# Moving three two-by-two up pairs one block earlier and giving their taps and gate product later

## The chip, the cores and the metric

The kernel runs on one core of one Trainium2 chip. The metric is the device time of one execution in microseconds; several executions are timed and their median is compared. One further execution is recorded by the hardware profiler, and all rows below come from that one.

## The reference, cut to what matters

The program is one block of a gated hybrid encoder on 512 positions of width 1024, all in float32. The change lies in the channel mixer at its end:

```python
h = rms_norm(x, norm_ffn_g[l])
up = causal_dwconv(h @ w_up[l], conv_ffn_w[l])      # w_up: 1024 x 5632, three taps per channel
a, b = jnp.split(up, 2, axis=-1)                    # two halves of 2816
x = x + (jax.nn.silu(a) * b) @ w_down[l]            # w_down: 2816 x 1024
...
return rms_norm(x, norm_f_g)
```

## The kernel before, in words

Everything is held transposed: 128 channels on the partitions, 512 positions along the row. Float32 products are made from three matmuls in a rounded format. Each weight chunk `raw` is read by DMA, ScalarE writes its rounded high part `wh` (L279), VectorE writes the rest `wl = raw - wh` (L283), and TensorE computes `wh*xh`, `wh*xl` and `wl*xh`. `split()` issues this for one chunk. There are two buffers for `wh` and two for `wl`, so the split of a chunk can start when TensorE has left the chunk two places before it. Five buffers hold `raw`.

The chunks are used in one fixed order, the list `stream`. `chunk.n` counts those that TensorE has been given, `len(parts)` those that have been split. The names in the list are `up<m>` (one plain up block of 128 columns, 48 matmuls), and `P<n>` and `F<n>` (the first and second part of one step of a two by two scheme with seven products, 18 and 24 matmuls).

The 5632 up columns are taken in pairs `j` = 0 to 21: block `2j` is a piece of `a`, block `2j+1` the piece of `b` that it is multiplied with. Most pairs are two plain up blocks (`block`, 96 matmuls). The pairs named in `UPS` go by the two by two scheme instead (`up_pair`): four chunks P, F, P, F with 84 matmuls, whose products land in four PSUM banks `us`, and five VectorE sums (L1099 to L1104) that put the two blocks together. The scheme needs weights that are sums of blocks; these are made in DRAM by a chain of six DMAs a group (copy, add, copy, add, copy, add: L140 on SyncE's queue, L143 on GpSimd's queue). The DMAs of all groups stand in the list `todo`, and `tick()` issues the next one; `ticks(name)` says how many go with the split of each chunk. The F chunks are then loaded from these sums. Pairs 0 to 11 are the first half, pairs 12 to 21 the second; after each half `down` multiplies what has been made with `w_down`.

After each block or pair, `up` scales the result by the norm (`z`, L1122 and L1120) and applies the three taps: a ScalarE copy (L615) and two VectorE additions (L616, L619) into a tile `fu`, of which there are three buffers. `glu` then applies SiLU to `a` (L1132) and multiplies by `b` on GpSimd: into `ge` for an even `j` (L1135) and into `go` for an odd `j` (L1142). After an odd `j`, the sums and splits of the result that `down` needs (L1152 to L1157, L1161, L1162) are put in the list `later` with a chunk at which they are due. `run_later` takes from that list at each split as much as a budget allows: 1.7 us at an up chunk, and 0.45 us at a P or F chunk of an up pair, which none of these entries fits. `flush()` issues what is left, and `glu` calls it for every odd `j`.

An instruction is put into its engine's queue by a planner, which takes among those ready by its own reckoning the one that stands first in the program. `keep` holds the order of matmuls and DMAs as written; `after_split()` puts what is issued under it behind the newest split on ScalarE and on VectorE. Each engine works its queue off strictly in order.

The last pair of `UPS` has a further duty: behind it the space of the x sums is free, the running result `x1` is read back into it (`xg`, L1109), and later pairs put `z` there (`fz`) and not in PSUM. A copy of a piece of `x1` (L1343) is queued on ScalarE behind that read.

Of the kernel before, what the change touches and what calls it, by code (L numbers as in the profile page):

```python
# [8 lines left out]
F32 = mybir.dt.float32  # L9
# [4 lines left out]
P = 128  # L14
D = 1024
S = 512
# [18 lines left out]
G1, G2, GF, BG, CM, CF, BF = 0, 8, 16, 24, 40, 52, 184  # L35
# [17 lines left out]
)  # L53
GS = 2
NFF = len(STEPS[0]) + len(STEPS[1])
UPS = (3, 7, 13, 16, 19)
NUP = NFF + 2 * (8 - GS)
MIXED = (4, 2, 4, 4, 2, 4, 2)

# [5 lines left out]
def block_kernel(ctx, tc, xT, vecs, wv, win, wmix, wo, wup, wst, wdp, outT):  # L65
# [56 lines left out]
    for (j0, j1), n0, n1 in zip(PHASES, (0, len(STEPS[0])), (len(STEPS[0]), NFF - 1)):  # L122
        groups += [[NUP + 2 * i, NUP + 2 * i + 1] for i, j in enumerate(UPS) if j0 <= j < j1]
        groups += [list(range(n, min(n + 2, n1))) for n in range(n0, n1, 2)]
    groups.append([NFF - 1])
    nstep = [len(d) for d in STEPS[0] + STEPS[1]] + [2] * (2 * (KB - GS) + 2 * len(UPS))
    todo = []
# [40 lines left out]
    def up_n(j):  # L168
        return [NUP + 2 * UPS.index(j) + d for d in range(2)]

# [14 lines left out]
    for ph, (j0, j1) in enumerate(PHASES):  # L185
        for j in range(j0, j1):
            if j in UPS:
                for m in up_n(j):
# [9 lines left out]
    raws, parts, order = [], [], {}  # L198
# [3 lines left out]
    def after_split():  # L202

        st = ExitStack()
        for ins in order.values():
            st.enter_context(tc.issue_after(ins))
        return st

    def load(upto):
        for k in range(len(raws), min(upto, len(stream) - 1) + 1):  # L210
            nm, src, ncol = stream[k]
            if held[0] == NRAW:
                return
            held[0] += 1
            raw = wp.tile([P, D], F32, tag="raw", name=f"raw_{nm}", bufs=NRAW)
            if k == 0:

                keep(nc.scalar.dma_start(raw[:, :VW], src[:, :VW]))
                keep(nc.sync.dma_start(raw[:, VW:ncol], src[:, VW:]))
            else:  # L220
                keep(nc.sync.dma_start(raw[:, :ncol], src))
            raws.append(raw[:, :ncol])
# [31 lines left out]
    def split(hl=None):  # L254

        k = len(parts)
        if k == len(stream):
            return
        nm, _, ncol = stream[k]
        load(k + (LOOK if k >= gs0 else AHEAD))  # L260
        if k >= gs0:
            for _ in range(ticks(nm)):
                tick()
        if hl is None:
            hl = []
            for x in "hl":
                if k == 0:
                    wp.tile([P, PADW[x]], F32, tag=f"pad{x}", name=f"pad_{x}")
                hl.append(wp.tile([P, D], F32R, tag=f"w{x}", name=f"w{x}_{nm}", bufs=2)[:, :ncol])
        hi, lo = hl  # L270
        raw = raws[k]
        if k < 2:
            if k:
                keep(nc.scalar.activation(hi[:, :VW], raw[:, :VW], AF.Copy))
            else:
                keep(nc.vector.tensor_copy(hi[:, :VW], raw[:, :VW]))
            keep(nc.vector.tensor_copy(hi[:, VW:], raw[:, VW:]))
        else:
            ins = nc.scalar.activation(hi, raw, AF.Copy)  # L279
            order["hi"] = ins.ins  # L280
            if k < KB:
                keep(ins)
        ins = nc.vector.tensor_sub(lo, raw, hi.bitcast(F32))  # L283
        order["lo"] = ins.ins
        if k < KB:
            keep(ins)
        held[0] -= 1
        parts.append((hi, lo))
        run_later(k, 0.45 if nm[0] in "PF" and int(nm[1:]) >= NUP else {"u": 1.7, "P": 1.6, "F": 0.75, "d": 0}.get(nm[0], 3.5))
# [323 lines left out]
    def taps(u, z, w):  # L613

        nc.scalar.activation(u, z, AF.Copy, scale=col(w + 2))  # L615
        nc.vector.scalar_tensor_tensor(  # L616
            u[:, 1:], z[:, : S - 1], col(w + 1), u[:, 1:], op0=ALU.mult, op1=ALU.add
        )
        nc.vector.scalar_tensor_tensor(  # L619
            u[:, 2:], z[:, : S - 2], col(w), u[:, 2:], op0=ALU.mult, op1=ALU.add  # L620
        )
# [116 lines left out]
    z, e, o = (ap.tile([n, S], F32, tag="pp", name=nm, bufs=NPP) for nm in ("fz", "fe", "fo"))  # L738
# [156 lines left out]
    for j in range(KB):  # L895
# [28 lines left out]
        a, b = gs  # L924
# [44 lines left out]
    def block(name, xh, xl, lead=False):  # L969
        wh, wl = chunk(name)  # L970
        q = acc(f"p_{name}")
        for kb in range(KB):
            ks = slice(kb * P, (kb + 1) * P)
            if lead and kb < 2:
                if kb:
                    passes([
                        (q[:, cs], 0, wh[:, b], wl[:, b], xh[:, a, cs], xl[:, a, cs], True, False)
                        for a, b in enumerate((slice(0, P), ks)) for cs in halves
                    ], 4)
                continue  # L980
            mm3(q, wh[:, ks], wl[:, ks], xh[:, kb, :], xl[:, kb, :], kb == 0, kb == KB - 1)
        return q
# [54 lines left out]
    nrm = {}  # L1037
# [13 lines left out]
    pu = lead(["up0", "up1"], x1h, x1l, mid)  # L1051
# [7 lines left out]
    fp = ctx.enter_context(tc.tile_pool(name="fp", bufs=1))  # L1059
# [13 lines left out]
    def fz(name):  # L1073
        fz.n += 2
        a = 2 * KB + fz.n % (2 * KB)
        return xg[:, a : a + 2].rearrange("p h c -> p (h c)")
# [11 lines left out]
    def up_pair(j):  # L1088
# [8 lines left out]
        with after_split():  # L1097
# [6 lines left out]
            nc.vector.tensor_add(p45h, p45h, u.unsqueeze(1).to_broadcast([P, 2, S // 2]))  # L1104
        if j == UPS[-1]:
            xg = xfp.tile([P, 4 * KB, 2 * P], F32, tag="xf", name="xg")
# [2 lines left out]
                nc.gpsimd.dma_start(x1[:, a : a + 4, :], x1d[:, a : a + 4, :])  # L1109
        return p23, p45  # L1110

    def up(j, rb2, pu=None):
        uu = []
        if j in UPS:
            pu = up_pair(j)
        for s_ in range(2):
            p = pu[s_] if pu else block(f"up{2 * j + s_}", x1h, x1l, True)
            z = p if j <= UPS[-1] else fz(f"fz{j}{s_}")
            if s_ and j in UPS:
                nc.vector.scalar_tensor_tensor(z, p, -1.0, rb2, op0=ALU.mult, op1=ALU.mult)  # L1120
            else:
                nc.vector.tensor_mul(z, p, rb2)  # L1122
            u = fp.tile([P, S], F32, tag="fu", name=f"fu{j}{s_}", bufs=3)
            taps(u, z, CF + 3 * (2 * j + s_))
            uu.append(u)
        return uu

    def glu(ph, j, uu):
        a, b = uu
        q, k = j // 2, len(parts) - 1  # L1130
        g0 = place(ph, q)
        nc.scalar.activation(a, a, AF.Silu)  # L1132
        if j % 2 == 0:
            ge = glu.even = fp.tile([P, 2, 2 * P], F32, tag="ge", name=f"ge{q}", bufs=2)
            keep(nc.gpsimd.tensor_mul(ge, a.rearrange(halves_of, h=2), b.rearrange(halves_of, h=2)))  # L1135
            return
        flush()
        ge = glu.even
        go = fp.tile([P, 6, 2 * P], F32, tag="gr", name=f"go{q}")

        def mul(eng):
            return eng.tensor_mul(go[:, 0:2, :], a.rearrange(halves_of, h=2), b.rearrange(halves_of, h=2))  # L1142

        if j + 1 < PHASES[ph][1]:
            keep(mul(nc.gpsimd))
        else:
            later.append((k + 3, 0.7, (("q", q),), lambda: mul(nc.vector)))
        b11, b12 = ge[:, 0, :], ge[:, 1, :]
        b21, b22, t1, t2, t3, t4 = (go[:, i, :] for i in range(6))

        def t13():
            nc.vector.tensor_sub(t1, b11, b12)  # L1152
            nc.vector.tensor_sub(t3, b22, b12)

        def t24():
            nc.vector.scalar_tensor_tensor(t2, t1, -1.0, b22, op0=ALU.mult, op1=ALU.subtract)
            nc.vector.scalar_tensor_tensor(t4, t2, -1.0, b21, op0=ALU.mult, op1=ALU.subtract)  # L1157

        def hl(src, gs):
            def f():  # L1160
                nc.scalar.activation(gh[:, gs, :], src, AF.Copy)  # L1161
                nc.vector.tensor_sub(gl[:, gs, :], src, gh.bitcast(F32)[:, gs, :])  # L1162

            return f


        d = (2, 3, 4) if j + 1 < PHASES[ph][1] else (4, 5, 6)
        w = [(d[0], 0.85, t13), (d[0], 0.85, t24), (d[1], 0.7, hl(ge[:, : 1 + ph, :], slice(g0, g0 + 1 + NF * ph, NF)))]
        w += [(d[x > 0 and 2 or 1], 0.7, hl(go[:, x : x + 2, :], slice(g0 + 1 + x, g0 + 3 + x))) for x in (0, 4, 2)]
        for n, us, f in w:  # L1170
            later.append((k + n, us, (("q", q),), f))
# [126 lines left out]
    for ph, (j0, j1) in enumerate(PHASES):  # L1298
        if ph:
            flush()  # L1300
            acc = ring(*X, *Y)
        for j in range(j0, j1):
            glu(ph, j, up(j, nrm["b"], None if j else pu))
        down(ph, ph * len(STEPS[0]))


# [210 lines left out]
```

## Time and profile before

| | |
|---|---|
| median of 3 runs | 694.88 us (693.62 to 694.9) |
| profiled execution | 693.69 us, of which the span from the first to the last instruction is 691.9 us |
| mean granted TensorE clock | 0.997 |
| busy: PE, DVE, ACT, POOL | 681.3, 548.3, 364.5, 184.6 us (98%, 79%, 53%, 27%) |
| PE waits recorded from the second half's first up block to the start of its `down` | 2.7, 0.4 and 0.2 us |

PE is TensorE, PEld its weight load, DVE VectorE, ACT ScalarE, POOL GpSimd, SP SyncE; a q behind the name means the engine's queue of DMAs and semaphores. Times in rows are us from the start of the span. A row of the timeline has the start, the length, the engine, the line, the operation, what it writes and reads, the tile sizes and how many instructions were merged; in brackets the idle time before it and what ended that. Instructions are pipelined, so the time that one of a row of equals really takes is the distance from its start to the next start, which is a little less than its length.

### The profile page before, as it was taken

To read this page: it belongs to the slowest core of one execution; us is meant where nothing else is said; L and a number is where in the kernel's file an instruction comes from. 1 tells how busy PE (TensorE), PEld (TensorE's weight loads), DVE (VectorE), ACT (ScalarE), POOL (GpSimd) and SP (SyncE) were. 2 spreads that over 40 slices of the span, in tenths; PEclk is the share of its full clock that TensorE was granted. 3 is DMA by queue.
4 is the path that set the end of the run, shared out by engine and by line. 5 is a ranking of instruction groups with operands and counts; after the bars stand their busy time and mean duration, and the time that the engine had idled before them with its cause. 6 is when DMAs were issued, how large, how long until landed. Compare 5 with 4: busy or idle time off the path is not lost.

```text
span 691.9 us, 14692 instructions
## 1 busy us (share of the span) xinstructions
PE 681.3 (98%) x5916; PEld 678.7 (98%) x5916; DVE 548.3 (79%) x864; ACT 364.5 (53%) x581; POOL 184.6 (27%) x209
## 2 busy tenths in 40 slices
PE   9999999999999999999999999999999999899996
PEld 9999999999999999999999999999999999899996
DVE  6678777886687777768887989978755899799886
ACT  6575556564564544446654535445443455355663
POOL 5123745444021010233403132330221323123000
PEclk9999999999999999999999999999999999999998
DMA  8626957478489796888975869679899968594623
GB/s 302 201 86 218 207 144 184 100 179 169 126 222 286 212 262 206 236 263 275 215 208 140 219 129 303 169 198 266 208 300 300 231 162 204 119 312 111 198 82 122
DMA packets 66117, 139.64 MB, mean 202 GB/s; under 512 B 5856, under 2 KB 30432, under 8 KB 65792
## 3 DMA queue, kind: packets, MB, share of 16 engines
q1 hardware_dynamic: 44592, 105.72, 46.8%
q0 software_dynamic: 20736, 32.28, 26.5%
q8 instruction: 46, 0.75, 0.4%
q10 hardware_dynamic: 720, 0.69, 0.3%
q14 instruction: 23, 0.19, 0.1%
HBM read 132.32 MB, written 49.81 MB: 263 GB/s over the span
## 4 chain that ended last, share of the span: by engine, by line
PE 86%; DVE 8%; ACT 3%; issue 2%; DMA 1%; ACTq 0%; SPq 0%; DVEq 0%
PE p_up L312 17%; PE p_in L312 14%; PE dn L330 13%; PE gs L330 8%; PE p_wo L312 6%; PE us L330 6%; PE p_up L330 5%; PE yc L330 3%; PE ya L312 3%; PE o L705 2%; PE pa L524 2%; PE pb L526 1%; PE tp L690 1%; PE pdB L312 1%; PE pdA L312 1%
## 5 line engine op out<-in xcount | busy, mean ns | idle before, releaser
L143 POOL DMA_DIRECT2D sum<-in_wst_dram x66 | 70.9, 1227 | 96.1 <-DMA sum<-sum 67.6
L312 PE MATMUL p_in<-xf,wh_in 128*128 128x256 f32 x576 | 95.7, 278 | 0.0
L312 PE MATMUL p_up<-x1h,wh_up 128*128 128x256 f32 x416 | 81.1, 276 | 0.0
L312 PEld LDWEIGHTS p_in<-xf,wh_in 128*128 128x128 f32 x576 | 80.4, 188 | 0.7
L312 PE MATMUL p_up<-x1h,wl_up 128*128 128x256 f32 x416 | 81.0, 276 | 0.0
L312 PE MATMUL p_up<-x1l,wh_up 128*128 128x256 f32 x416 | 81.0, 276 | 0.0
L279 ACT ACTIVATE wh_F<-raw_F 128x1024 fp32r<-128x1024 f32 (+1 forms) x42 | 44.2, 1052 | 65.0 <-PE ya L312 25.8
L283 DVE TENSOR_TENSOR wl_F<-raw_F,wh_F 128x1024 fp32r<-128x1024 f32 (+1 forms) x42 | 53.5, 1275 | 28.6 <-ACT wh_F L279 28.3
L312 PEld LDWEIGHTS p_up<-x1h,wh_up 128*128 128x128 f32 x416 | 62.7, 188 | 0.0
L312 PEld LDWEIGHTS p_up<-x1h,wl_up 128*128 128x128 f32 x416 | 62.6, 188 | 0.0
L312 PEld LDWEIGHTS p_up<-x1l,wh_up 128*128 128x128 f32 x416 | 62.6, 188 | 0.0
L312 PE MATMUL p_in<-xf,wl_in 128*128 128x256 f32 x288 | 56.6, 278 | 0.1
L279 ACT ACTIVATE wh_P<-raw_P 128x768 fp32r<-128x768 f32 (+1 forms) x42 | 35.1, 836 | 39.6 <-PE p_up L312 17.9
L279 ACT ACTIVATE wh_up<-raw_up 128x1024 fp32r<-128x1024 f32 x34 | 35.9, 1057 | 28.6 <-PE p_up L312 14.1
L283 DVE TENSOR_TENSOR wl_up<-raw_up,wh_up 128x1024 fp32r<-128x1024 f32 x34 | 42.3, 1244 | 9.5 <-ACT wh_up L279 9.4
L283 DVE TENSOR_TENSOR wl_P<-raw_P,wh_P 128x768 fp32r<-128x768 f32 (+1 forms) x42 | 40.1, 956 | 11.5 <-ACT wh_P L279 6.0
L312 PEld LDWEIGHTS p_in<-xf,wl_in 128*128 128x128 f32 x288 | 43.6, 188 | 0.3 <-DVE wl_in L283 0.3
L1135 POOL TENSOR_TENSOR ge<-fu,fu 128x512 f32<-128x512 f32 x11 | 20.1, 1825 | 82.3 <-DVE fu L619 44.7
L330 PE MATMUL dn<-gh,wh_F 128*128 128x256 f32 x156 | 36.5, 277 | 0.4 <-ACT wh_F L279 0.4
L330 PE MATMUL dn<-gl,wh_F 128*128 128x256 f32 x156 | 36.4, 276 | 0.0
L283 DVE TENSOR_TENSOR wl_in<-raw_in,wh_in 128x1024 fp32r<-128x1024 f32 x24 | 30.2, 1257 | 6.1 <-ACT wh_in L279 3.4
L1142 POOL TENSOR_TENSOR go<-fu,fu 128x512 f32<-128x512 f32 x9 | 12.6, 1396 | 72.9 <-DVE fu L619 54.5
(361 smaller groups left out, 2122.1 us busy)
## 6 DMA issues: line engine op xcount, KB each, us to landing
raw_F<-sum SPq DMA_DIRECT2D x41, 512.0 KB, 5.4
raw_up<-in_wup_dram SPq DMA_DIRECT2D x34, 512.0 KB, 5.4
raw_P<-in_wst_dram SPq DMA_DIRECT2D x41, 384.0 KB, 5.1
raw_in<-in_win_dram SPq DMA_DIRECT2D x24, 512.0 KB, 3.6
sum<-in_wst_dram POOLq DMA_DIRECT2D x41, 256.0 KB, 6.9
sum<-in_wst_dram SPq DMA_DIRECT2D x20, 512.0 KB, 8.6
sum<-in_wst_dram POOLq DMA_DIRECT2D x20, 512.0 KB, 9.1
sum<-sum SPq DMA_DIRECT2D x40, 256.0 KB, 6.2
```

The lines of the kernel that those rows point to most:

```text
L143: return lambda: keep(nc.gpsimd.dma_start(dst, src, accum_op=ALU.add))
L279: ins = nc.scalar.activation(hi, raw, AF.Copy)
L283: ins = nc.vector.tensor_sub(lo, raw, hi.bitcast(F32))
L312: keep(nc.tensor.matmul(out[:, cs], w, x[:, cs], start=start and i == 0 and c == 0, stop=stop and i == 2 and c == len(cut) - 1,))
L330: keep(nc.tensor.matmul(out, wl if x == 1 else wh, xl if x == 2 else xh, start=opens and bk not in seen, stop=closes and bk not in left,))
L524: keep(nc.tensor.matmul(pa[t][:, :VW], xt, w[:, :VW], start=start, stop=stop))
L526: keep(nc.tensor.matmul(pb[t], xt, w[:, VW:], start=start and t % 2 == 0, stop=stop and t % 2 == 1))
L690: keep(nc.tensor.transpose(tp[:, ks], pt[:, ks], ident))
L705: keep(nc.tensor.matmul(o[:, os_], vv[:, kb, pr, e, :], x[:, kb, cs], start=e == 0 and kb == 0 and i == 0, stop=e == 1 and kb == nk - 1 an ...
L1135: keep(nc.gpsimd.tensor_mul(ge, a.rearrange(halves_of, h=2), b.rearrange(halves_of, h=2)))
L1142: return eng.tensor_mul(go[:, 0:2, :], a.rearrange(halves_of, h=2), b.rearrange(halves_of, h=2))
```

## The change

Three things are changed. In the second half the pairs that go by the two by two scheme are 12, 15 and 18 and no longer 13, 16 and 19; so four plain blocks stand between two of them as before, none stands ahead of the first, and six stand behind the last. For these three pairs, `up` makes `z` (in PSUM, in place) and stops; taps, SiLU and the gate product are put in `held_up`. They are issued in the next pair's `up`, behind its first block's matmuls, after splits have been issued up to the third chunk behind the up pair, and behind that split on ScalarE and VectorE. And `glu` is called from inside `up`.

```diff
-UPS = (3, 7, 13, 16, 19)
+UPS = (3, 7, 12, 15, 18)
...
-    def up(j, rb2, pu=None):
+    def up(ph, j, rb2, pu=None):
         uu = []
         if j in UPS:
             pu = up_pair(j)
         for s_ in range(2):
             p = pu[s_] if pu else block(f"up{2 * j + s_}", x1h, x1l, True)
+            if s_ == 0 and held_up:
+                while len(parts) < chunk.n + 2:
+                    split()
+                with after_split():
+                    held_up.pop()()
             z = p if j <= UPS[-1] else fz(f"fz{j}{s_}")
             if s_ and j in UPS:
                 nc.vector.scalar_tensor_tensor(z, p, -1.0, rb2, op0=ALU.mult, op1=ALU.mult)
             else:
                 nc.vector.tensor_mul(z, p, rb2)
-            u = fp.tile([P, S], F32, tag="fu", name=f"fu{j}{s_}", bufs=3)
-            taps(u, z, CF + 3 * (2 * j + s_))
-            uu.append(u)
-        return uu
+            if j not in UPS or not ph:
+                z = tapped(j, s_, z)
+            uu.append(z)
+        if j in UPS and ph:
+            held_up.append(lambda: glu(ph, j, [tapped(j, s_, z) for s_, z in enumerate(uu)]))
+        else:
+            glu(ph, j, uu)
+
+    held_up = []
+
+    def tapped(j, s_, z):
+        u = fp.tile([P, S], F32, tag="fu", name=f"fu{j}{s_}", bufs=3)
+        taps(u, z, CF + 3 * (2 * j + s_))
+        return u
...
         for j in range(j0, j1):
-            glu(ph, j, up(j, nrm["b"], None if j else pu))
+            up(ph, j, nrm["b"], None if j else pu)
```

## The prediction

> **What bounds the kernel now.** I read the page's busy shares first, then the chain of work that ended last over the second half's up blocks, then TensorE's (PE's) waits there.
>
> ```profile
> PE 681.3 (98%) x5916; PEld 678.7 (98%) x5916; DVE 548.3 (79%) x864; ACT 364.5 (53%) x581; POOL 184.6 (27%) x209
> ```
> ```profile
> 523.84 1.36 PE p_up L330 x12
> ...
> 600.70 9.52 PE us L330 x84
> ...
> 632.31 1.37 PE dn L330 x12
> ```
> ```profile
> PE p_up L330 <- DVE wl_up L283: 2.7, 1, 2.7
> ```
> PE is the bound: an undisturbed up pair takes 9.52 us for 84 matmuls, 0.1133 us each. The stage from 523.84 to 632.31 has 14 plain blocks of 48 and three pairs of 84, 924 matmuls, so 104.7 us of work; it lasts 108.5. About 3.75 us are lost in it. PE's timeline shows where:
>
> ```profile
> 567.77 0.28 PE L330 MATMUL us<-xf,wl_P 128*128 128x256 f32 x1
> 568.22 0.39 PE L330 MATMUL us<-x1h,wh_F 128*128 128x256 f32 x1 [0.17 <-ACT wh_F L279]
> 587.50 0.28 PE L330 MATMUL p_up<-x1l,wh_up 128*128 128x256 f32 x1
> 590.43 0.75 PE L330 MATMUL p_up<-x1h,wl_up 128*128 128x256 f32 x4 [2.65 <-DVE wl_up L283]
> 591.02 0.28 PE L312 MATMUL p_up<-x1h,wh_up 128*128 128x256 f32 x1
> 627.17 0.28 PE L330 MATMUL p_up<-x1l,wh_up 128*128 128x256 f32 x1
> 627.41 0.73 PE L330 MATMUL p_up<-x1h,wl_up 128*128 128x256 f32 x4
> 633.51 0.84 PE L330 MATMUL dn<-gh,wl_P 128*128 128x256 f32 x6
> 634.79 0.39 PE L330 MATMUL dn<-gh,wh_F 128*128 128x256 f32 x1 [0.44 <-ACT wh_F L279]
> ```
> Starts stand 2.93 us apart at 587.50 where 0.11 would do; with the slower restart (0.59 us for four) this stop costs 2.96. The others cost 0.45 (568.22), 0.25 (627.41, with its restart) and 0.7 (634.79, just behind the stage). Together 4.4 us: all that can be won here. The large one is at up36, the third block behind pair 16. VectorE's (DVE's) queue, and the split's ScalarE (ACT) half, say why:
>
> ```profile
> 577.50 0.42 DVE L1099 TENSOR_TENSOR uz<-us,uz 128x256 f32<-128x256 f32 x1
> 577.83 0.68 DVE L1162 TENSOR_TENSOR gl<-ge,gh 128x512 fp32r<-128x512 f32 x1
> 578.43 0.42 DVE L1100 TENSOR_TENSOR uu<-us,uz 128x256 f32<-128x256 f32 x1
> ...
> 582.69 0.69 DVE L1122 TENSOR_TENSOR p_up<-p_up,rb_n 128x512 f32<-128x512 f32 x1
> 583.28 1.40 DVE L616 SCALAR_TENSOR_TENSOR fu<-us,vec,fu 128x511 f32<-128x511 f32 x2
> 584.60 1.40 DVE L619 SCALAR_TENSOR_TENSOR fu<-us,vec,fu 128x510 f32<-128x510 f32 x2
> 585.91 0.74 DVE L616 SCALAR_TENSOR_TENSOR fu<-p_up,vec,fu 128x511 f32<-128x511 f32 x1
> ...
> 589.16 1.21 DVE L283 TENSOR_TENSOR wl_up<-raw_up,wh_up 128x1024 fp32r<-128x1024 f32 x1
> 590.30 0.74 DVE L616 SCALAR_TENSOR_TENSOR fu<-p_up,vec,fu 128x511 f32<-128x511 f32 x1
> ```
> ```profile
> 581.51 1.06 ACT L279 ACTIVATE wh_up<-raw_up 128x1024 fp32r<-128x1024 f32 x1 [2.98 <-issue]
> ```
> The high part was there at 582.57, yet DVE first did 582.69 to 589.16: the pair's four taps (583.28 to 585.91, 2.63 us), other taps and gate work. DVE is full for long:
>
> ```profile
> 544.10:566.10 22.00, 22.00 (x197) 22.00 (x196) 21.24 (x32) 10.15 (x16) 5.41 (x4) 1.00 0.82 204
> 576.00:600.60 24.60, 21.95 (x193) 21.75 (x193) 21.31 (x33) 10.49 (x17) 5.27 (x5) 1.00 0.59 127
> ```
> (The columns are stretch, length, and busy PE, PEld, DVE, ACT, POOL; then clock and DMA.) In the four blocks behind a pair, 21.8 us of PE work, DVE has 21.2 and 21.3 us of its own. So order within DVE's queue decides.
>
> **The change, part by part.** No matmul is added or removed; the granted clock is 1.00 in these rows. Undisturbed, pair 12 would run 523.84 to 533.36, four blocks to 555.12, pair 15 to 564.64, four blocks to 586.40, pair 18 to 595.92 and six blocks to 628.56.
>
> *The held taps.* The third block's split now stands ahead of the pair's taps and of all that follows them. At up36 that alone puts `wl` at some 582.7 and ready by 583.9, when it is first used about 587.8. I take the 2.96 us as gone (bounds: all of it, or all but 0.3, since the pair's own 2.63 are surely out of the way). This adds a wait: DVE can't touch the taps until the third block's high part is made. That part ends 5.44 + 1.06 = 6.5 us behind the pair. Pair 16, which ended at 576.0, had its sums begun 1.5 behind that (577.50); sums and products took 5.2 to 582.69 with three `gl` of 0.60 among them (577.83 to 578.43), 3.4 without. So behind pair 12 DVE stands idle about 1.6 us; behind 15 and 18 gate sums fill that. It costs nothing, since no gate sums are due in the four blocks behind pair 12; without that cover the first split of pair 15 would be up to 1.6 late. Queued behind are only taps, whose results nothing on PE needs before `down`; the banks they leave late (two of eight) are taken again a pair later.
>
> *The fourth block.* Its split comes behind the held taps and one block's `z` and taps: with 0.60 and 0.66 each (starts 582.69, 583.28, 584.60) that is some 4.5 us behind the third split, so ready about 1.6 us ahead of use. Nothing lost; two late microseconds would cost 0.4.
>
> *Six plain blocks at the end.* DVE gets 32.6 us behind pair 18 where it had 21.8 behind pair 19, with the same work. The stops at 627.41 and 634.79 (0.95 us) should go. The cover is slack in DVE; without it both stay.
>
> *Pair 12 first.* Its loads move ahead by two chunks; its sums' last DMA is still issued some 24 chunks earlier. Four split pieces and `combine`'s last five small sums fall into 9.5 us of an otherwise empty DVE: nothing.
>
> *Where it hurts: pair 18.* The gate sums of pairs 12/13 come due at chunks of pair 15, where the budget of 0.45 us takes none, so they wait for up32 and up33. Those of 14/15 come due at pair 18's chunks and are flushed by `glu(17)`, ahead of pair 18's first split P40. So two gate loads fall between pairs 15 and 18; between pairs 13 and 16 there was one.
>
> ```profile
> 539.71 2.17 DVE L283 TENSOR_TENSOR wl_F<-raw_F,wh_F 128x1024 fp32r<-128x1024 f32 x1 [0.44 <-ACT wh_F L279]
> ...
> 564.88 0.94 DVE L283 TENSOR_TENSOR wl_P<-raw_P,wh_P 128x768 fp32r<-128x768 f32 x1
> 565.75 0.74 DVE L619 SCALAR_TENSOR_TENSOR fu<-p_up,vec,fu 128x510 f32<-128x510 f32 x1
> ...
> 574.90 0.41 DVE L1152 TENSOR_TENSOR go<-ge 128x256 f32<-128x256 f32 x1
> 575.24 0.41 DVE L1153 TENSOR_TENSOR go<-go,ge 128x256 f32<-128x256 f32 x1
> ```
> ```profile
> 539.51 1.29 POOL L1135 TENSOR_TENSOR ge<-fu,fu 128x512 f32<-128x512 f32 x1 [10.40 <-DVE fu L619]
> ```
> Work between up32's split (high part ready at 561.92 + 1.06, about 563.0) and the end of P40's: four splits of 1.14 (589.16 to 590.30) and one of 0.87 (564.88 to 565.75), 5.4; two gate loads of four sums at 0.34 and four `gl` at 0.60, 7.5; pair sums and two products 3.4 (577.50 to 582.69 less three `gl`); pair taps 2.6; three `z` at 0.60 and six taps at 0.66, 5.8. Sum 24.7, so 587.7. P40's rest is wanted after 12 of its matmuls, 586.40 + 1.36 = 587.76. No slack; on top come up35's `z` (0.6, its bank is full by then) and collisions with GpSimd: a split of usually 1.23 us took 2.17 while a gate product ran, 0.94 more, and two products (`go` 15, `ge` 16) fall into this stretch. I take one collision: a new stop of 1.5 us; bounds 0 (no collision, no `z`) and 3.4 (both, so 2.4, and 1.0 where F40's high part has to queue behind a late SiLU, as the one at 568.22 may have).
>
> The Trainium skill ("SBUF — State Buffer", section "SBUF: two separate sides") says that VectorE with two SBUF inputs and GpSimd lock the port pair they share, and that the loser blocks for the whole instruction. The 2.17 us split agrees: it came 0.2 us behind the product and lasted until 1.1 us behind its end. By that rule both products would cost their full 1.29 here; the new stop would be 3.1 us and the time 693.6.
>
> *x1's read.* It moves from the end of pair 19, 610.2, to that of pair 18, 595.9.
> ```profile
> 621.23 0.42 ACT L1343 ACTIVATE gh<-xg 128x256 fp32r<-128x256 f32 x1 [2.53 <-DMA xg<-x1d]
> ```
> ACT stood 2.53 us in front of that copy. The wait will come again, some 14 us sooner; taps are behind it, and six blocks cover them: 0, or 0.9 if it delays up41's split past its slack of 1.6.
>
> *Sum.* 4.4 won, 1.5 lost: 2.9 us. The profiled execution was 693.69 us, 1.8 over its span; it would be 690.8. The median, 694.88, lies 1.2 above it; less 2.9 that is **692.0 us**.
>
> **Rivals.** *The stop only moves.* All of the upper bound at pair 18, plus the late read: 4.4 - 3.4 - 0.9, so 694.8. For it: DVE has as much work as before, and two gate loads meet. Against: one gate load ahead of pair 16 cost 0.45 at 568.22, and the second one has 9.5 us of pair 15 in which DVE can catch up on all else.
>
> *The full lock.* Both products, 2 x 1.29 (539.51), block DVE for their whole length in the stretch that has no slack: 587.7 + 0.6 + 2.6 is 3.1 late, 4.4 - 3.1 won, 693.6. The rule of the Trainium skill's page above is this case. Against: the one row that shows it has 0.94 and not 1.29.
>
> *It doesn't do what it says:* the planner queues other work ahead of the third split. No change, 694.9. Against: the split now stands first in the program, and ACT's half was on time at 582.57.
>
> *Slower.* GpSimd (POOL) works its queue in order. The last sum DMAs of the groups behind pair 18's move up to three chunks later, and the held `go` 15 product is now behind them. Each such add waits for a copy to land.
> ```profile
> POOL sum L143 <- DMA sum<-sum: 67.6, 6, 22.1
> ```
> The last of them waits for a copy that SyncE issues behind the load of P40, when F39's split has freed a buffer, near 562. `fu` has three buffers, so up33's taps wait for `go` 15, and ACT and DVE queue P40's split behind those taps. From about 578 on each late microsecond costs one; 16 us are there, but 22.1 has been waited. At 22 the stop grows by 6: 698. Pair 18's own sums, whose last add comes near 560, are wanted only at 586.
>
> **How the numbers follow.** Chances: forecast 0.65, stop moves 0.13, lock 0.09, nothing done 0.05, slower 0.08. A measurement of this kernel tells 0.2% (1.4 us) from no change: 693.5 divides faster from same. The forecast's cases are nearly all faster, the three after it mostly same. The forecast's own bounds: 4.4 won without a new stop, 690.5, and 694.88 - 1.0 = 693.9. One run in three stood 1.3 below the median, so I reach to 689.8 below and, towards the stop that moves, to 694.6 above.
>
> **What the profile would show.** Right: PE's wait for `wl_up` at the third block gone behind all three pairs, the pair's L616 and L619 behind a `wl_up`, stage end near 630 and no wait at `down`'s first F; a stop of one to two microseconds at P40. Wrong: a stop at P40 or F40 above 3 us, POOL waiting in L143 ahead of `go`, or a DVE idle behind each pair for the held split.

## The result, and the profile after

The changed kernel takes 690.71 us (median; 690.7 to 691.35) against 694.9 us for the kernel before beside it (693.62 to 695.24). The ratio is 0.9944, 95% interval 0.993 to 0.9959. The profiled execution took 690.7 us with a span of 688.9, against 693.69 and 691.9. So the profiles differ by 3.0 us and the medians by 4.2: two amounts, with two causes.

The busy shares, the chain that ended last over the second half's `up` and its `down`, and PE's waits there, all of the kernel after:

```profile
PE 680.0 (99%) x5916; PEld 677.8 (98%) x5916; DVE 547.3 (79%) x864; ACT 364.6 (53%) x581; POOL 184.2 (27%) x209
```
```profile
523.78 9.52 PE us L330 x84
...
555.07 6.13 PE us L330 x54
561.22 1.07 ACT wh_up L279
...
577.22 1.31 POOL go L1157
...
587.72 0.88 DVE wl_P L283
588.65 8.45 PE us L330 x72
...
629.74 15.30 PE dn L330 x135
```
```profile
PE us L330 <- DVE wl_P L283: 0.9, 1, 0.9
```
The stage now lasts from 523.78 to 629.74, 105.96 us; before it lasted 108.47. The single recorded wait for `wl_up` at the third block behind a pair is gone. In its place stands one shorter wait at P40, pair 18's first chunk. From 629.74 `down` runs 135 matmuls without a break, so the stop at its first F is gone as well. The chain tells where the new wait comes from: between 561.22 and 588.65 it leaves PE and runs through DVE for the most part, with pieces on ACT and one product on POOL. In that stretch DVE's queue sets the end, and elsewhere in the stage PE does.

PE at the new stop and where the fourth block behind pair 18 first uses its low part, and DVE's queue at three places (behind pair 12, ahead of P40, behind pair 18):

```profile
587.32 0.39 PE L330 MATMUL us<-xf,wh_P 128*128 128x256 f32 x2
588.65 0.50 PE L330 MATMUL us<-x1h,wl_P 128*128 128x256 f32 x2 [0.94 <-DVE wl_P L283]
...
614.16 0.62 PE L330 MATMUL p_up<-x1h,wl_up 128*128 128x256 f32 x4
```
```profile
538.78 0.70 DVE L1127 TENSOR_TENSOR p_up<-p_up,rb_n 128x512 f32<-128x512 f32 x1 [0.25 <-PE p_up L312]
539.87 1.23 DVE L283 TENSOR_TENSOR wl_up<-raw_up,wh_up 128x1024 fp32r<-128x1024 f32 x1 [0.39 <-ACT wh_up L279]
...
577.60 0.75 DVE L619 SCALAR_TENSOR_TENSOR fu<-p_up,vec,fu 128x510 f32<-128x510 f32 x1
578.25 1.35 DVE L283 TENSOR_TENSOR wl_up<-raw_up,wh_up 128x1024 fp32r<-128x1024 f32 x1
...
582.11 1.22 DVE L1168 TENSOR_TENSOR go<-go,ge 128x256 f32<-128x256 f32 x1
...
587.64 0.95 DVE L283 TENSOR_TENSOR wl_P<-raw_P,wh_P 128x768 fp32r<-128x768 f32 x1
588.51 0.69 DVE L1127 TENSOR_TENSOR p_up<-p_up,rb_n 128x512 f32<-128x512 f32 x1
...
603.89 1.22 DVE L283 TENSOR_TENSOR wl_up<-raw_up,wh_up 128x1024 fp32r<-128x1024 f32 x1
605.02 1.29 DVE L1177 TENSOR_TENSOR gl<-go,gh 128x512 fp32r<-128x512 f32 x2
606.23 1.41 DVE L616 SCALAR_TENSOR_TENSOR fu<-us,vec,fu 128x511 f32<-128x511 f32 x2
607.54 1.40 DVE L619 SCALAR_TENSOR_TENSOR fu<-us,vec,fu 128x510 f32<-128x510 f32 x2
...
610.12 2.22 DVE L619 SCALAR_TENSOR_TENSOR fu<-xg,vec,fu 128x510 f32<-128x510 f32 x1
...
612.25 1.21 DVE L283 TENSOR_TENSOR wl_up<-raw_up,wh_up 128x1024 fp32r<-128x1024 f32 x1
```
The two rows at 606.23 and 607.54 are the pair's own taps. They now stand behind the third block's split (603.89), where before they stood ahead of it. Two matmuls from 587.32 on end the first 12 of P40; the next would start at 587.55 and starts at 588.65. With its slower restart (0.34 us for two where 0.23 would do) the stop costs 1.2 us.

### The profile page after: what moved, and what is told of

It is laid out like the page before. It is cut to its first block, busy times and chain, and to the rows that moved or that the text cites. A ratio compares the mean times of both kernels' runs of the same rounds, so it can differ in the third digit from the quotient of the medians.

```text
span 688.9 us, 14690 instructions
## 1 busy us (share of the span) xinstructions
PE 680.0 (99%) x5916; PEld 677.8 (98%) x5916; DVE 547.3 (79%) x864; ACT 364.6 (53%) x581; POOL 184.2 (27%) x209
## 4 chain that ended last, share of the span: by engine, by line
PE 89%; DVE 6%; ACT 2%; issue 2%; DMA 1%; ACTq 0%; POOL 0%; SPq 0%; DVEq 0%; POOLq 0%
PE p_up L312 18%; PE p_in L312 14%; PE dn L330 13%; PE gs L330 8%; PE p_wo L312 6%; PE us L330 6%; PE p_up L330 6%; PE yc L330 3%; PE ya L312 3%; PE o L705 2%; PE pa L524 2%; PE pb L526 1%; PE tp L690 1%; PE pdB L312 1%; PE pdA L312 1%
## 5 line engine op out<-in xcount | busy, mean ns | idle before, releaser
L143 POOL DMA_DIRECT2D sum<-in_wst_dram x66 | 70.8, 1163 | 122.3 <-DMA sum<-sum 93.0
L279 ACT ACTIVATE wh_in<-raw_in 128x1024 fp32r<-128x1024 f32 x24 | 25.3, 1056 | 10.8 <-issue 3.4
```

Source lines behind the costliest of these rows:

```text
L143: return lambda: keep(nc.gpsimd.dma_start(dst, src, accum_op=ALU.add))
```

## The experiments

**What makes the median slower than the profile?** The kernel before, unchanged, profiled again:

> The kernel before, unchanged, for a second profile. The first profile of before was 693.69 us while its median is 694.9; the changed kernel's profile and median are both 690.7. So of the 4.2 us between the medians the two profiles show only 3.0. Theory: the missing 1.2 us is a further or longer stop of TensorE in the second half's up blocks, where VectorE has no slack; a profile near 694.9 shows stops of about 5.6 us there and not 4.4. Rival: it lies elsewhere (the start, the first half, the end) and the stops there are again 4.4 us. Time: 693.6 to 695.2 by both.

Measured: 694.93 us (693.27 to 697.11), ratio 1.0004 [0.999, 1.0018]; the profiled execution took 694.82 us, 1.1 more than the one in the prediction. PE's row at the stop, and a window behind it (columns as in the prediction's windows); then the same window in the first profile of the same kernel:

```profile
590.34 0.74 PE L330 MATMUL p_up<-x1h,wl_up 128*128 128x256 f32 x4 [2.68 <-DVE wl_up L283]
```
```profile
591.80:595.20 3.40, 3.40 (x18) 3.40 (x18) 2.20 (x6) 0.00 (x0) 2.32 (x3) 0.51 0.36 135
```
```profile
591.80:595.20 3.40, 3.40 (x32) 3.40 (x31) 2.17 (x6) 0.00 (x0) 2.23 (x3) 1.00 0.40 139
```
No stop is longer: 2.68 us idle at up36 against 2.65. So the longer stop that was expected isn't there. But 1.5 us behind that stop the granted clock falls to 0.51 for 3.4 us, and 18 matmuls run where 32 ran in the first profile. Fourteen matmuls at 0.1133 are 1.6 us. The executions fall into two groups to match: of 56 of this kernel, 16 took 693.15 to 693.81, with a mean granted clock of 0.997 or 0.998 over the whole execution, and the other 40 took 694.4 or more, 38 of them at 0.994 to 0.996. A stretch of 3.4 us at half clock is 0.0025 of the span, which is the distance between the two clocks. The execution that the prediction was worked out on belongs to the smaller group.

**Does the stretch at half clock follow from the stop?** Ten matmuls with zero weights, which add 0 to the bank, go into the stop of the kernel before; the stop's end stays with DVE:

```diff
-    def passes(prods, lead):
+    def passes(prods, lead, fill=0):
...
+            if x == 1:
+                for _ in range(fill):
+                    keep(nc.tensor.matmul(out, zw, xh, start=False, stop=False))
+                fill = 0
...
-            p = pu[s_] if pu else block(f"up{2 * j + s_}", x1h, x1l, True)
+            p = pu[s_] if pu else block(f"up{2 * j + s_}", x1h, x1l, True, NFILL if 2 * j + s_ == 36 else 0)
```

> The kernel before, with ten extra matmuls of zero weights put into up36 at the place where TensorE stops for 2.9 us; they add 1.13 us of TensorE work inside that stop and 0 to the result. Theory (the stop itself costs 2.9 us, and in two executions of three its 2.8 us of idle time also halve TensorE's granted clock for some 3.4 us, which costs another 1.2 us or more): the stop is 1.7 us idle, the granted clock stays 1.00, all executions lie near 693.3 and none at 694.6 or above; median 693.0 to 693.7. Rival (the slower executions have another cause than the length of the idle time): the upper group stays in about two of three, median 694.6 to 695.

Measured: 693.38 us (692.69 to 694.36; nine of eleven at 693.53 or below), ratio 0.9983 [0.9974, 0.9993]. PE's rows and the same window of this kernel:

```profile
587.51 1.36 PE L332 MATMUL p_up<-x1h,zw 128*128 128x256 f32 x10
590.35 0.74 PE L335 MATMUL p_up<-x1h,wl_up 128*128 128x256 f32 x4 [1.48 <-DVE wl_up L284]
```
```profile
591.80:595.20 3.40, 3.40 (x32) 3.40 (x31) 2.18 (x6) 0.00 (x0) 2.31 (x3) 1.00 0.39 141
```
The work goes on at 590.35, when it did without them (590.34), so nothing is saved in the stop itself. Its idle part fell from 2.68 to 1.48 us, the clock in the window stays at 1.00, all eleven executions have a mean clock of 0.997 to 0.999, and the group at 694.4 and above is gone. So the half clock is a consequence of the idle time. This part of the gain is shown by taking it alone: 1.5 us in the medians (694.89 to 693.38).

**The places alone.** The kernel before with `UPS = (3, 7, 12, 15, 18)` and no held taps:

```diff
-UPS = (3, 7, 13, 16, 19)
+UPS = (3, 7, 12, 15, 18)
```

> Only the first part of the change: pairs 12, 15 and 18, with taps and gate products given at once as before. Theory (order in VectorE's queue makes the large stop, and the later place of taps takes it away): the stop of about 3 us comes back at a third block behind a pair, up34 or up40, and the time is 693.5 to 695. Rival (where the pairs stand makes the gain, by the six blocks behind the last one): about 691, no stop above 1.5 us.

Measured: 692.65 us (691.9 to 694.23), ratio 0.9975 [0.9963, 0.9987], profiled 692.02. Its waits and DVE's queue:

```profile
PE p_up L330 <- DVE wl_up L283: 2.6, 1, 2.6
```
```profile
603.08 1.40 DVE L616 SCALAR_TENSOR_TENSOR fu<-us,vec,fu 128x511 f32<-128x511 f32 x2
...
608.23 1.94 DVE L283 TENSOR_TENSOR wl_up<-raw_up,wh_up 128x1024 fp32r<-128x1024 f32 x1
```
The long stop is back at the third block, now of pair 18 (up40), with the pair's taps ahead of the split. It is a little below what was expected because the small stops went. Its executions fall into two groups again, six at 691.9 to 692.3 and six at 693.0 to 694.2 (five of these at a mean clock of 0.995 or 0.996, all others at 0.998), with 2.6 us of idle.

**The hold alone.** The kernel after with the pairs left at 13, 16 and 19:

```diff
-UPS = (3, 7, 12, 15, 18)
+UPS = (3, 7, 13, 16, 19)
```

> Only the second part: pairs 13, 16 and 19 as before, with taps and gate products held. Theory (the held taps are the gain, and a stop of 1.2 us remains where two gate loads meet): no stop at up36, the two gate loads now meet ahead of pair 19 or behind it, one or two small stops of 1 to 2 us in all, 690.5 to 692. Rival (the place of the pairs is needed): 693 or more, with stops at the first steps of down, since only four blocks follow pair 19.

Measured: 690.54 us (690.42 to 690.88), ratio 0.9939 [0.9922, 0.9955]. Its waits and DVE's queue at the start of `down`:

```profile
PE dn L330 <- DVE wl_P L283: 0.9, 1, 0.9
```
```profile
627.95 1.88 DVE L1177 TENSOR_TENSOR gl<-go,gh 128x512 fp32r<-128x512 f32 x3
...
629.76 0.95 DVE L283 TENSOR_TENSOR wl_P<-raw_P,wh_P 128x768 fp32r<-128x768 f32 x1
```
The hold alone gives the whole gain. One stop of 0.9 us idle is left, in `down`'s first P, behind three `gl` of the last gates; the waits at the last block and at `down`'s first F are gone here too, with four blocks behind the last pair. Moving the pairs as well leaves one stop of the same size at P40 in its place: 690.54 against 690.71.

**The third split behind the taps again.** The kernel after, with the splits ahead of the held taps cut by one:

```diff
-                while len(parts) < chunk.n + 2:
+                while len(parts) < chunk.n + 1:
```

> The changed kernel with the held taps issued behind the split of the second block that follows, not the third. Theory (the third block's split must stand ahead of the taps): VectorE's queue behind pair 18 is then that of the run with the pairs moved only, so a stop of about 2.8 us at up40 returns and the time is about 692 to 694. Rival (any later place will do, since the pair's taps are only 2.6 us): no stop at up40 above 0.5 us, 690.4 to 691.

Measured: 693.74 us (691.97 to 695.69), ratio 0.9982 [0.9972, 0.9993]. DVE's queue behind pair 18, and the wait:

```profile
PE p_up L330 <- DVE wl_up L283: 2.4, 1, 2.4
```
```profile
603.18 1.40 DVE L616 SCALAR_TENSOR_TENSOR fu<-us,vec,fu 128x511 f32<-128x511 f32 x2
604.49 1.40 DVE L619 SCALAR_TENSOR_TENSOR fu<-us,vec,fu 128x510 f32<-128x510 f32 x2
...
608.33 1.71 DVE L283 TENSOR_TENSOR wl_up<-raw_up,wh_up 128x1024 fp32r<-128x1024 f32 x1
```
With 2.6 us of taps back ahead of the split, the stop at up40 is back with 2.39 us idle. The place of this one split in DVE's queue is what the change works by; that the taps wait a block is not. Seven of the twelve executions stand at 693.67 and above with a mean clock of 0.994 to 0.996, the rest at 692.49 or below with 0.998: a stop of 2.4 us idle goes with the second group too.

**The stop at P40.** If two gate loads between pairs 15 and 18 make it, it goes when one of them is done elsewhere. First attempt: the chunks of all three pairs of the second half, 12, 15 and 18, get the usual budget for gate sums; only those of pairs 3 and 7, which are numbered `NUP` to `NUP + 3`, keep the small one:

```diff
-        run_later(k, 0.45 if nm[0] in "PF" and int(nm[1:]) >= NUP else {...}.get(nm[0], 3.5))
+        run_later(k, 0.45 if nm[0] in "PF" and NUP <= int(nm[1:]) < NUP + 4 else {...}.get(nm[0], 3.5))
```

> The changed kernel, but the budget of 0.45 us at the chunks of an up pair is lifted to that of other P and F chunks (1.6 and 0.75 us) for the second half's pairs, so that the gate sums of 12/13 go out while pair 15 runs, where VectorE has some 5 us idle. Theory (the one stop left, 1.2 us at P40 of pair 18, comes from two gate loads between pairs 15 and 18): the stop goes, 689.4 to 689.8. Rival (the stop is the price of the collision with GpSimd's product and of the order at P40, whatever was done earlier): stop as before within 0.3, 690.4 to 691.

Measured: 690.75 us (690.66 to 691.23), ratio 0.9942 [0.9927, 0.9958], so no better than the change. PE's wait, DVE's queue, and the product on POOL that one of DVE's sums waits for:

```profile
PE us L330 <- DVE wl_F L283: 0.3, 1, 0.3
```
```profile
585.85 0.94 DVE L283 TENSOR_TENSOR wl_P<-raw_P,wh_P 128x768 fp32r<-128x768 f32 x1
...
592.79 0.42 DVE L1168 TENSOR_TENSOR go<-go,ge 128x256 f32<-128x256 f32 x1 [1.19 <-POOL go L1157]
...
594.40 1.22 DVE L283 TENSOR_TENSOR wl_F<-raw_F,wh_F 128x1024 fp32r<-128x1024 f32 x1
```
```profile
590.88 1.87 POOL L1157 TENSOR_TENSOR go<-fu,fu 128x512 f32<-128x512 f32 x1 [8.03 <-DVE fu L619]
```
P40's split stands 1.8 us sooner (585.85 against 587.64) and its stop is gone. But gate sums also went between pair 18's own splits, where one waits 1.19 us for POOL with F41's split behind it. By this run's chain PE loses 0.8 us at F41, and 0.5 at F39 in pair 15, among whose splits the first gate load now stands; together that is what P40's stop had cost. So the time is the rival's, though P40's stop did go.

Second attempt: pair 18 as in the change, and the usual budget at the first three chunks of pair 15:

```diff
-        run_later(k, 0.45 if nm[0] in "PF" and int(nm[1:]) >= NUP else {...}.get(nm[0], 3.5))
+        run_later(k, 0.45 if nm[0] in "PF" and int(nm[1:]) >= NUP and nm not in ("P38", "F38", "P39") else {...}.get(nm[0], 3.5))
```

> As the run with the lifted budget, but lifted for P38, F38 and P39 of pair 15 alone, so that no gate sum gets between the splits of pair 18 (there the sums of 16/17 waited for GpSimd's product and made a new stop of 0.6 us at F41). Theory: P40 without a stop and none at F41, one of up to 0.3 at F39; 689.6 to 690.1. Rival (VectorE's total work in this stretch sets the time, and a stop taken away comes back somewhere behind): 690.4 to 690.9, with a stop of 0.5 us or more at another chunk.

Measured: 689.92 us (689.88 to 690.29), ratio 0.9936 [0.9923, 0.9949], profiled 689.92. The chain from the first pair to `down`, and three rows of DVE:

```profile
523.77 9.52 PE us L330 x84
...
555.05 8.61 PE us L330 x76
...
563.69 1.21 PE us L330 x8
...
586.79 9.52 PE us L330 x84
...
628.95 16.09 PE dn L330 x142
```
```profile
552.07 0.42 DVE L1167 TENSOR_TENSOR go<-ge 128x256 f32<-128x256 f32 x1
...
560.12 2.38 DVE L1177 TENSOR_TENSOR gl<-go,gh 128x512 fp32r<-128x512 f32 x2
...
585.93 0.94 DVE L283 TENSOR_TENSOR wl_P<-raw_P,wh_P 128x768 fp32r<-128x768 f32 x1
```
The first gate load now begins at 552, ahead of the crowded stretch, and P40's split stands 1.7 us sooner. Pairs 12 and 18 run without a break in PE's chain. Pair 15 doesn't: two `gl` of that gate load stand ahead of F39's split and take 2.38 us (other rows have 1.29 for two), while a product runs on POOL (559.47, for 1.89 us), and F39's last 8 matmuls take 1.21 us in the chain where 0.91 would do. Pair 18 starts at 586.79, which is 0.46 later than an undisturbed pair and four blocks (31.28 us) behind 555.05. That is the small stop at F39 that was expected, somewhat larger. The stage is 105.18 us long, where its 924 matmuls need 104.7. It is the quickest of the kernels run: 0.8 below the change's median, with no execution in common, although the two ratios' intervals overlap.

## Why the prediction was right, and where it was not

*The bound and the held taps: right.* DVE's order was the cause. Putting the split behind the taps again brings the stop back (2.39 us idle), and the hold without the new places gives the whole gain.

*The idle DVE behind pair 12: over-sized, harmless.* The split stands 6.57 us behind the pair's end (533.30 to 539.87), as worked out. DVE is idle for 0.25 and 0.39 us there and not for 1.6, because its sums and the first block's `z` (538.78) fill the rest. It costs nothing, as forecast.

*The fourth block: no cost, but less than half the slack.* Behind pair 18 its split ends at 613.46 and PE uses the low part at 614.16: 0.7 us ahead and not 1.6. The 1.6 doesn't follow from the terms shown for it. With the third split begun 6.5 us behind the pair, two splits of 1.14 and the 4.5 us between them, the low part is ready 13.3 behind the pair and used three blocks and eight matmuls behind it, at 17.2: that is 3.9 us. What stood between the two splits took 7.2 us and not 4.5 (605.02 to 612.25): two `gl` that the sum left out took 1.2, and the slow tap at 610.12 took 1.5 more than others. The third split itself began 0.3 later, 6.8 behind the pair's end at 597.10. The slack was left by luck.

*Six blocks at the end, and pair 12 first: right in effect.* No stop is recorded at the last block, at `down`'s first F, or in pair 12. But the prediction took the slack that six blocks give DVE for the cover of both, and with the hold alone and four blocks both are gone too (0.9 us idle at `down`'s first P in their place).

*Pair 18: right in kind and place, 1.2 us where 1.5 was said.* DVE finished P40's split at 588.59. Without the collisions (0.80 and 0.13, see *The full lock* below) that is 587.66, where the sum of work gave 587.7. That the two meet is partly luck: up32's high part was ready at 562.29 (561.22 + 1.07) and not at 563.0, and the work from there took 25.4 us and not 24.7. The two collisions add 0.93, where the prediction took one of 0.94. The term that was wrong is up35's `z`: it stands behind P40's split (588.51), so its 0.6 us isn't paid. Against that, PE wanted the low part 0.2 us sooner by its rows (587.55, not 587.76) and restarted 0.1 slower.

*x1's read: right.* ACT waits for it at 608, 1.59 us, and PE has no stop behind it:

```profile
608.03 0.42 ACT L1358 ACTIVATE gh<-xg 128x256 fp32r<-128x256 f32 x1 [1.59 <-DMA xg<-x1d]
```

*The sum: right; the step to the median: wrong.* The profiled execution was to lose 2.9 us and lost 3.0; the stop at P40 was 0.3 smaller than taken, and 0.2 of that isn't seen in the span, because the time behind DVE's last sums is 0.3 longer (3.7 us for 3.4), which no run here explains. The step that failed is "The median, 694.88, lies 1.2 above it; less 2.9". The 1.2 us was carried over as if it were a constant. It was itself a consequence of the stop: 40 of 56 executions were in the longer group, and in the one of them that was profiled the clock halved behind the stop. With the stop the longer group went, and filling the stop alone takes it away. A median that lies above the profile of the same kernel, with the runs in two groups, was a sign that the profile shown lacked something that most executions had; the prediction saw the one lower run, used it for the width of its range, and did not ask for the cause.

*The rivals.* "The stop only moves" is refuted by size: 1.2 us at P40 in place of 4.4. "Does nothing" is refuted by the wait that went. "Slower" didn't come about; these are POOL's rows:

```profile
571.11 1.02 POOL L143 DMA_DIRECT2D sum<-in_wst_dram  x1 [4.35 <-DMA sum<-sum]
...
577.22 1.30 POOL L1157 TENSOR_TENSOR go<-fu,fu 128x512 f32<-128x512 f32 x1 [5.08 <-DVE fu L616]
...
581.75 1.30 POOL L1150 TENSOR_TENSOR ge<-fu,fu 128x512 f32<-128x512 f32 x1 [3.23 <-DVE fu L619]
...
610.00 1.78 POOL L1150 TENSOR_TENSOR ge<-fu,fu 128x512 f32<-128x512 f32 x1
```
POOL did wait in L143 ahead of `go` 15 (4.35 us), which the prediction named as a sign of being wrong. But the adds of the sums were done at 572.13, and `go` 15 then waited 5.08 us for the taps that it reads, not for them. The link that this rival feared is in the chain all the same (the product at 577.22), so by these rows adds more than 5.08 us later would have made the stop longer; no run tried that.

*The full lock* has the right mechanism and the wrong price. The row at 582.11 begins 0.36 us into the product of 581.75 and ends at 583.33, 0.28 behind its end (583.05), taking 1.22 us where its like take 0.42. The Trainium skill ("SBUF — State Buffer", section "SBUF: two separate sides") says that whichever of the two starts later is blocked until the earlier is through, when VectorE reads two SBUF inputs; the trace agrees. But the price is at most what is left of the other instruction: 0.94 us were left at 582.11, and the row took 0.80 more than its like, not 1.29. The product at 577.22 met mostly a `z` and a tap that read one input from PSUM, and cost 0.13 (the split of 578.25, 1.35 for 1.22).

## What to carry to other kernels

Where an in-order engine makes operands for the bounding engine and also clears up behind it, list what stands in its queue between an operand's being possible and its being done; move the clearing-up behind the operand before moving anything else. Then add up the queue's work up to the next deadline, since a stop taken away at one place can return at the next crowded stretch, here each time smaller (2.96, 1.2 and 0.46 us). And where executions fall into two groups, find which one the profile belongs to before a difference of profiles is taken for a difference of medians.

## What the runs showed of the hardware that was not expected

*A stop can cost more than its length.* Behind 2.7 us of idle PE the granted clock fell to 0.51 for 3.4 us in one of two profiled executions of the kernel before; the times and mean clocks of most of its executions fit the same. With 2.6 and 2.4 us idle (the places alone; the third split behind the taps) about half of the executions stand in an upper group, nearly all with the lower mean clock; no execution of that group was profiled there. With 1.5 us or less (the filled stop, and the four kernels with the hold and its split ahead) no such group shows. The Trainium skill ("TensorE: Matmul & The Clock Gate", section "Part 1: The HAM clock gate (the "warmup" mystery)") puts the fall to half rate behind an idle window of about 3.4 us that runs freely, and the return to the full rate behind a busy window of the same length. The rate and the length of the slow stretch agree; the limit doesn't, since 2.7 us were enough here. Why some executions of the same kernel escape isn't settled; a window that starts at another moment in each would explain it, but no run here shows one.

*Where an operand lies matters for collisions.* For pair 19, `z` is put in SBUF (`xg`), and its tap at 610.12 took 2.22 us beside POOL's product at 610.00; the tap of `p_up` at 577.60, which reads PSUM, took 0.75 beside the product at 577.22. The slow tap cost nothing, because the split behind it was still done 0.7 us ahead of its use.
